# One token tile of an output projection computed by column halves, its second-norm row finished after the expert threshold search, and the route stage ordered by hand

## The chip, the cores and the metric

The kernel runs on one core of one Trainium2 chip. The metric is the device time of one execution in microseconds (us), lower is better. A core has five engines with a queue of instructions each: TensorE (PE in the profile; its weight loads are PEld), VectorE (DVE), ScalarE (ACT), GpSimd (POOL) and SyncE (SP, which here only issues DMAs). Each works through its own queue in order; semaphores tie the queues together.

## The reference, cut to what matters

One layer over 2048 tokens of width 1024, in fp32: a modulated RMS norm, a combined input projection, a convolution half and a neighbourhood-attention half, the output projection with a gated residual, a second modulated RMS norm, and sixteen expert-choice SwiGLU experts of which each takes the 256 tokens with the highest affinity.

```
x = x + g1 * (concatenate([y_conv, y_attn], -1) @ w_out)
h2 = modulate(rms_norm(x, norm_ffn_g), sh2, sc2)           # h * (1 + scale) + shift
aff = softmax(h2 @ w_router)                               # 2048 x 16
wts, tok = top_k(swapaxes(aff, 1, 2), 256)                 # per expert
xs = h2[tok]
y = (silu(xs @ w_gate) * (xs @ w_up)) @ w_down * wts
x = x + g2 * zeros.at[tok].add(y);  out = rms_norm(x, norm_final_g)
```

## The kernel before, in words

`run` calls the stages in turn: `in_proj` (norm, input projection, convolution), `attention`, `route_consts`, `out_proj`, `route`, `moe`. Each matrix product is made of fp32 values split into a high part (a cast, on ACT) and a low part (a subtraction, on DVE or POOL), so that three matmuls stand for one.

**out_proj** goes over 16 token tiles of 128 tokens. `tile_mm(t)` loads the tile of x, runs 48 matmuls of 512 columns into a PSUM tile `po` of two banks (8 slices k, for each of two column halves: high by high, high by low, low by high), multiplies by the gate `rb[:, 0]`, adds x and stores the row tile to `acc`. `norm2(t)` squares with a row sum on ACT (into the tile `h2`) and makes the reciprocal root on POOL (`rstd`, six small instructions). `tail(t)` transposes the tile (eight transposes on TensorE), splits it into `h2h` and `h2l`, and after every second tile runs 16 gate matmuls of 256 columns and makes logits `lg`. `store_h2(t)` scales, adds the shift (`rb[:, 1]`) and stores the row tile to `h2d` in DRAM, from which the experts gather. `soft` makes the softmax of a stretch of slots of `lg`: seven pairs of tiles in the last loop step, the eighth at the end.

**route** transposes the affinities into `pa`, takes a copy `af` and a bf16 copy `afh`, and finds each expert's threshold in 30 steps of a bit search (the loop in L1093 to L1103: a compare with count on DVE, a matmul, three small DVE instructions). Then two masks, a running count `cum`, two transposes into `pt`, and the copy into `slot`.

**moe** goes over 16 experts in 24 chunks of weights each. `prep(e)` makes one-hot tiles from `slot` (16 compares), sums token numbers with them on TensorE, writes `idx`, and has POOL gather rows of `h2d` into `xr` by indirect DMA. `load(i)` brings one megabyte of weights into `raw` (three buffers) from SP and splits it into `whi` and `wlo`; for the first three loads the subtraction is POOL's. `gather` transposes `xr` into the experts' input. The stage begins with `load(0)`, `load(1)`, `load(2)`, `prep(0)` and the four parts of `gather(0)`.

**What sets the order.** The framework's scheduler orders each engine's queue. It plays the program through with its own costs: an engine that is free takes, among the instructions that are ready, the one that stands first in the program; a DMA keeps its issuing engine occupied for the transfer. Inside `tc.manual_schedule(engines=...)` the named engines take that stretch's instructions in program order. That holds for all of `attention`, for ACT, DVE and TensorE (`MAIN`) in `in_proj`, and for POOL (`ENG`) in moe until the fourth chunk. Tiles come from pools that are opened and closed like a stack: `rp` (the route pool, open from before attention to the end), p3a and p3 (attention), p4 (out_proj), p5 (route), p6 (moe, opened when p5 is closed). An instruction waits for the last user of the memory that its tile takes over.

Of the kernel before, what the change touches and what calls it, by code (L numbers as in the profile page):

```python
# [123 lines left out]
class Net:  # L124
# [727 lines left out]
    def out_proj(self):  # L852
        nc, tc, A, S = self.nc, self.tc, self.A, self.S
        with ExitStack() as es:
# [75 lines left out]
            def tile_mm(t):  # L930
# [4 lines left out]
                order = [4, 5, 6, 7, 0, 1, 2, 3]  # L935
                for ki, k in enumerate(order):
                    wh, wl = wo[k]
                    for n in range(2):
                        c = slice(n * 512, (n + 1) * 512)
                        nc.tensor.matmul(po[:, n], hi[:, k], wh[:, c], start=(ki == 0), stop=False)  # L940
                        nc.tensor.matmul(po[:, n], hi[:, k], wl[:, c], start=False, stop=False)
                    for n in range(2):
                        c = slice(n * 512, (n + 1) * 512)
                        nc.tensor.matmul(po[:, n], lo[:, k], wh[:, c], start=False, stop=(ki == KT - 1))
# [3 lines left out]
                sm = [SM[0][:, i, t % 2:t % 2 + 1] for i in range(3)]  # L948
# [4 lines left out]
                XT[t] = (xt, h2, sm, SM[0])  # L953
# [15 lines left out]
            def tail(t):  # L969
                xt, _, _, sm = XT[t]  # L970
                if t % 2 == 0:
                    R[0] = pool.tile([P, KT, W2], F32R, name="h2h", bufs=1)
                    R[1] = pool.tile([P, KT, W2], F32R, name="h2l", bufs=1)
                hh, hl = R[0], R[1]
                q = slice((t % 2) * P, (t % 2 + 1) * P)
                for a in range(2):
                    tp = ps.tile([P, 4, P], F32, name="tp4", bufs=2)
                    for k in range(4):
                        nc.tensor.transpose(tp[:, k, :], xt[:, (4 * a + k) * P:(4 * a + k + 1) * P], self.ident)
                    nc.scalar.copy(hh[:, 4 * a:4 * a + 4, q], tp)  # L980
                    nc.vector.tensor_sub(hl[:, 4 * a:4 * a + 4, q], tp, hh[:, 4 * a:4 * a + 4, q].bitcast(F32))
                if t % 2:
                    pr = ps.tile([2 * E, W2], F32, name="pr")
                    for k in range(KT):
                        nc.tensor.matmul(pr, wrs[:, k], hh[:, k], start=(k == 0), stop=False)
                        nc.tensor.matmul(pr, wrs[:, k], hl[:, k], start=False, stop=(k == KT - 1))
                    lt = pool.tile([2 * E, W2], F32, name="lt", bufs=1)
                    nc.scalar.copy(lt, pr)
                    tl = ps.tile([P, 2, 2, E], F32, name="tl", tag="tl")
                    for i in range(2):  # L990
                        nc.tensor.transpose(tl[:, i].rearrange("p a e -> p (a e)"), lt[:, i * P:(i + 1) * P],
                                            self.ident[:2 * E, :2 * E])
                    lg = self.lg[:, :, t // 2, :]
                    nc.scalar.copy(lg, tl[:, :, 0, :])
                    nc.vector.tensor_add(lg, lg, tl[:, :, 1, :])
                    nc.vector.tensor_mul(lg, lg, sm[:, 1, :, None].to_broadcast([P, 2, E]))
                    nc.vector.tensor_add(lg, lg, lsh[:, None, :].to_broadcast([P, 2, E]))
# [4 lines left out]
            for t in range(NT):  # L1002
                if t % 2 == 0 and t + 2 < NT:
                    ln_a(t // 2 + 1)
                tile_mm(t)
                if t % 2 == 1 and t + 1 < NT:
                    ln_b(t // 2 + 1)
                if t + 1 < NT:
                    ysplit(t + 1)
                if t < NT - 1:  # L1010
                    norm2(t)
                if t:
                    tail(t - 1)
                    store_h2(t - 1)
                if t == NT - 1:
                    self.soft(0, NT // 2 - 1)
            norm2(NT - 1)
            tail(NT - 1)
            self.soft(NT // 2 - 1, NT // 2)
            store_h2(NT - 1)  # L1020

    def route_pool(self, es):
# [5 lines left out]
        self.iob = p.tile([P, CAP], BF16, name="iob")  # L1028

# [44 lines left out]
    def route(self):  # L1074
        nc, tc, A, S = self.nc, self.tc, self.A, self.S
        with ExitStack() as es:
            pool = es.enter_context(tc.tile_pool(name="p5", bufs=1, reuse_waits="tile"))
# [45 lines left out]
            nc.vector.tensor_copy(self.slot.rearrange("p c e -> p (c e)"), pt.rearrange("p b t -> p (b t)"))  # L1123
# [261 lines left out]
```

## Time and profile before

| what | us |
|---|---|
| median of 3 runs | 3349.62 (3347.95 to 3350.89) |
| the profiled execution, whole | 3349.36 |
| its span, first to last instruction | 3347.6 |
| TensorE busy in the span | 3244.6 (97%) |
| DVE busy | 2339.9 (70%) |
| ACT busy | 1659.5 (50%) |
| POOL busy | 414.1 (12%) |

Times in the profile count from the start of the span. In the timeline each row has start, length, engine, source line, operation, output and inputs, and in square brackets how long the engine had been idle and what ended the wait; rows of the same kind that follow each other on an engine are merged (x3). The mean granted clock of TensorE over the span was 0.984 of full speed.

### The profile page before, as it was taken

How to read it: one execution, taken by the hardware profiler on the slowest of the kernel's cores; microseconds unless marked ns; L12 is line 12 of the kernel's file. 1: busy time of each engine (PE TensorE's matmuls, PEld its weight loads, DVE VectorE, ACT ScalarE, POOL GpSimd, SP SyncE). 2: the span in 40 equal slices, each digit the busy share in tenths (PEclk: the TensorE clock that was granted, in tenths of full speed). 3: DMA queues.
4: the chain of work that ended last, by engine and by line, in shares of the span. 5: the costliest groups of instructions: out<-in, count | busy, mean ns of one | idle time of the engine just before them, and what ended most of it. 6: DMA issues, size and time to landing. Idle time of an engine off the chain costs nothing. (4 is left out here: it accounts for less than half of the span.)

```text
span 3347.6 us, 47930 instructions
## 1 busy us (share of the span) xinstructions
PE 3244.6 (97%) x18394; PEld 2751.2 (82%) x18394; DVE 2339.9 (70%) x3637; ACT 1659.5 (50%) x2784; POOL 414.1 (12%) x739
## 2 busy tenths in 40 slices
PE   7999998999999699999999999999999999999998
PEld 4788887999777588888888888888888888888786
DVE  6798987998666776566665766756666566575666
ACT  7211124889433355454554555545545455454554
POOL 3100002444211200000000000000000000001221
PEclk9999998999999699999999999999999999999999
DMA  6243329996433466555565555665556556556765
GB/s 233 76 135 130 112 96 241 258 239 158 147 131 109 168 218 210 193 202 198 200 210 197 198 200 196 208 201 198 196 199 211 196 196 213 187 205 226 265 246 193
DMA packets 159585, 635.61 MB, mean 190 GB/s; under 512 B 47926, under 2 KB 62678, under 8 KB 106108
## 3 DMA queue, kind: packets, MB, share of 16 engines
q1 hardware_dynamic: 138172, 542.68, 46.1%
q0 software_dynamic: 21184, 89.86, 11.1%
q8 instruction: 145, 2.38, 0.3%
q14 instruction: 84, 0.69, 0.1%
HBM read 560.38 MB, written 72.10 MB: 189 GB/s over the span
## 5 line engine op out<-in xcount | busy, mean ns | idle before, releaser
L1227 PE MATMUL pgu<-xt,whi 128*128 128x512 f32 x4096 | 1446.1, 398 | 0.5 <-DVE xt L1197 0.5
L208 DVE TENSOR_TENSOR wlo<-raw,whi 128x1024 fp32r<-128x1024 f32 x762 | 918.9, 1220 | 648.6 <-ACT whi L207 647.2
L1228 PE MATMUL pgu<-xt,wlo 128*128 128x256 f32 x4096 | 1150.3, 281 | 1.4 <-DVE wlo L208 1.4
L207 ACT CAST whi<-raw 128x1024 fp32r<-128x1024 f32 x768 | 793.0, 1050 | 564.2 <-PE py L1263 278.4
L1227 PEld LDWEIGHTS pgu<-xt,whi 128*128 128x128 f32 x4096 | 769.8, 188 | 187.9 <-DVE xt L1197 0.9
L1228 PEld LDWEIGHTS pgu<-xt,wlo 128*128 128x128 f32 x4096 | 774.5, 189 | 2.9 <-DVE wlo L208 2.3
L1259 PE MATMUL py<-whi,hh 128*128 128x512 f32 x1024 | 405.9, 396 | 0.0
L1260 PE MATMUL py<-wlo,hh 128*128 128x512 f32 x1024 | 400.3, 391 | 0.0
L1263 PE MATMUL py<-whi,hl 128*128 128x512 f32 x1024 | 315.9, 390 | 0.0
L528 DVE SCALAR_TENSOR_TENSOR cacc<-v,k,cacc 128x2048 f32<-128x2048 f32 x120 | 281.5, 2346 | 1.6
L1232 ACT COPY gt<-pgu 128x256 f32<-128x256 f32 x512 | 188.9, 369 | 177.6 <-PE pgu L1228 177.6
L465 PE MATMUL mm<-hhi,whi 128*128 128x512 f32 x576 | 227.6, 395 | 0.0
L1263 PEld LDWEIGHTS py<-whi,hl 128*128 128x128 f32 x1024 | 192.4, 188 | 41.6
L467 PE MATMUL mm<-hhi,wlo 128*128 128x512 f32 x576 | 224.8, 390 | 0.0
L1259 PEld LDWEIGHTS py<-whi,hh 128*128 128x128 f32 x1024 | 192.7, 188 | 39.0 <-issue 0.2
L466 PE MATMUL mm<-hlo,whi 128*128 128x512 f32 x576 | 224.7, 390 | 0.0
L1260 PEld LDWEIGHTS py<-wlo,hh 128*128 128x128 f32 x1024 | 192.8, 188 | 38.2 <-issue 0.2
L1233 DVE TENSOR_TENSOR gt<-pgu,gt 128x256 f32<-128x256 f32 x512 | 213.5, 417 | 7.0 <-ACT gt L1232 6.9
L207 ACT CAST hh<-sl 128x256 fp32r<-128x256 f32 x256 | 104.1, 407 | 224.2 <-DVE sl L1236 223.8
L1315 POOL DMA_INDIRECT acc<-y,idx x28 | 51.9, 1854 | 1261.9 <-DVE y L1313 1184.9
L728 DVE CUSTOM_DVE_ANT_0 pt<-sp,bi 128x640 f32<-128x640 f32 (+1 forms) x128 | 113.5, 887 | 29.4 <-PE sp L721 27.8
L208 DVE TENSOR_TENSOR hl<-sl,hh 128x256 fp32r<-128x256 f32 x256 | 108.8, 425 | 34.1 <-ACT hh L207 7.1
(307 smaller groups left out, 4121.8 us busy)
## 6 DMA issues: line engine op xcount, KB each, us to landing
raw<-w_gu SPq DMA_DIRECT2D x256, 1024.0 KB, 4.8
raw<-w_dn SPq DMA_DIRECT2D x128, 1024.0 KB, 4.8
bi<-bias SPq DMA_DIRECT2D x14, 960.0 KB, 4.9
wm<-wm POOLq DMA_DIRECT2D x24, 512.0 KB, 4.2
vb<-vd SPq DMA_DIRECT2D x119, 96.0 KB, 9.5
wraw<-w_in SPq DMA_DIRECT2D x20, 512.0 KB, 4.5
kh<-kh POOLq DMA_DIRECT2D x16, 576.0 KB, 9.4
kl<-kl POOLq DMA_DIRECT2D x16, 576.0 KB, 10.6
```

The source lines that it names most:

```text
L207: nc.scalar.copy(hi, full)
L208: (eng or nc.vector).tensor_sub(lo, full, hi.bitcast(F32))
L465: nc.tensor.matmul(ps, w[0][:, k, :], h[0][:, k, :], start=(k == 0), stop=False)
L466: nc.tensor.matmul(ps, w[0][:, k, :], h[1][:, k, :], start=False, stop=False)
L467: nc.tensor.matmul(ps, w[1][:, k, :], h[0][:, k, :], start=False, stop=(k == KT - 1))
L528: nc.vector.scalar_tensor_tensor(acc, v[:, w:w + T], cwt[:, j, w:w + 1], acc, op0=OP.mult, op1=OP.add)
L1227: nc.tensor.matmul(p_, hi[:, a, k], xt[:, k, :], start=(k == 0), stop=False)
L1228: nc.tensor.matmul(p_[:, :CAP], lo[:, a, k], xt[:, k, :CAP], start=False, stop=(k == KT - 1))
L1233: nc.vector.tensor_add(t[:, a], pg[a][:, :CAP], t[:, a])
L1259: nc.tensor.matmul(py[e][a][b], hh[:, sa], hi[:, ff, sb], start=(f == 0), stop=False)
L1260: nc.tensor.matmul(py[e][a][b], hh[:, sa], lo[:, ff, sb], start=False, stop=False)
L1263: nc.tensor.matmul(py[e][a][b], hl[:, sa], hi[:, ff, sb], start=False, stop=(f == 15))
```

## The change

The last token tile's projection is computed by column halves: all of k for the first 512 columns into one PSUM tile, then the eight transposes of the tile before it, then all of k for the other 512 into a second PSUM tile. The functions are cut up for that (`proj`, `tile_in`, `flip`, `gates`, `logits`), and a new `last_pair` writes out the order of the last two tiles for TensorE, DVE and ACT. The square of the last tile is taken by halves. Its second-norm row is scaled into a tile `h3` while the last softmax runs; the shift is added and the row stored to `h2d` in `route`, after the search, and the tile `shift` moves with `h3` into the route pool (8 KB of a partition). `route` is ordered by hand too: `afh` is copied ahead of `af`, and the copy into `slot` goes to ACT. `soft` takes each step for both halves of the batch. The DMA descriptor scratch is set to 4096 bytes.

```diff
-            rb = pool.tile([P, 3, D], F32, name="rb")
-            for i in range(3):
-                nc.sync.dma_start(rb[:, i], S["rows"][i:i + 1, :].to_broadcast([P, D]))
+            rb = pool.tile([P, 2, D], F32, name="rb")
+            for i, r in enumerate((rb[:, 0], self.shift, rb[:, 1])):
+                nc.sync.dma_start(r, S["rows"][i:i + 1, :].to_broadcast([P, D]))
...
+            def proj(po, hi, lo, n):
+                order = [4, 5, 6, 7, 0, 1, 2, 3]
+                for ki, k in enumerate(order):
+                    wh, wl = wo[k]
+                    for m in n:
+                        c = slice(m * 512, (m + 1) * 512)
+                        nc.tensor.matmul(po[:, m], hi[:, k], wh[:, c], start=(ki == 0), stop=False)
+                        nc.tensor.matmul(po[:, m], hi[:, k], wl[:, c], start=False, stop=False)
+                    for m in n:
+                        c = slice(m * 512, (m + 1) * 512)
+                        nc.tensor.matmul(po[:, m], lo[:, k], wh[:, c], start=False, stop=(ki == KT - 1))
...
-                for c in ((slice(0, 512), slice(512, D)) if t == NT - 1 else (slice(0, D),)):
-                    nc.vector.tensor_mul(h2[:, c], po.rearrange("p a b -> p (a b)")[:, c], rb[:, 0, c])
-                    nc.vector.tensor_add(xt[:, c], xt[:, c], h2[:, c])
+            def tile_mm(t):
+                xt, hi, lo, po, h2 = tile_in(t)
+                proj(po, hi, lo, (0, 1))
+                nc.vector.tensor_mul(h2, po.rearrange("p a b -> p (a b)"), rb[:, 0])
+                nc.vector.tensor_add(xt, xt, h2)
...
-                nc.vector.scalar_tensor_tensor(h2, xt, sm[1], rb[:, 2], op0=OP.mult, op1=OP.mult)
-                nc.vector.tensor_add(h2, h2, rb[:, 1])
+                nc.vector.scalar_tensor_tensor(h2, xt, sm[1], rb[:, 1], op0=OP.mult, op1=OP.mult)
+                nc.vector.tensor_add(h2, h2, self.shift)
...
+            def flip(t, a):
...
+                return lambda: nc.vector.tensor_sub(hl[:, 4 * a:4 * a + 4, q], tp, hh[:, 4 * a:4 * a + 4, q].bitcast(F32))
+
+            def gates(pr, ks, kinds=(0, 1)):
+                for k in ks:
+                    for z in kinds:
+                        nc.tensor.matmul(pr, wrs[:, k], R[z][:, k], start=(k == 0 and z == 0),
+                                         stop=(k == KT - 1 and z == 1))
...
+            def last_pair():
+                t = NT - 1
+                xt, hi, lo, po, h2 = tile_in(t)
+                sm = XT[t][2]
+                sq = pool.tile([P, 2], F32, name="sq")
+                c = [slice(0, 512), slice(512, D)]
+
+                def square(q):
+                    nc.scalar.activation(h2[:, c[q]], xt[:, c[q]], AF.Square, accum_out=sq[:, q:q + 1])
+
+                def half(po, q):
+                    nc.vector.tensor_mul(h2[:, c[q]], po[:, q], rb[:, 0, c[q]])
+                    nc.vector.tensor_add(xt[:, c[q]], xt[:, c[q]], h2[:, c[q]])
+
+                proj(po, hi, lo, (0,))
+                for a in range(2):
+                    flip(t - 1, a)()
+                half(po, 0)
+                square(0)
+                po1 = ps.tile([P, 2, 512], F32, name="po", bufs=2)
+                proj(po1, hi, lo, (1,))
+                store_h2(t - 1)
+                self.soft(0, NT // 2 - 1)
+                low0 = flip(t, 0)
+                half(po1, 1)
+                nc.sync.dma_start(S["acc"][t * P:(t + 1) * P], xt)
+                square(1)
+                low0()
+                pr = ps.tile([2 * E, W2], F32, name="pr")
+                low1 = flip(t, 1)
+                gates(pr, range(KT // 2))
+                nc.vector.tensor_add(sm[0], sq[:, 0:1], sq[:, 1:2])
+                nc.vector.tensor_scalar(sm[0], sm[0], 1.0 / D, EPS, op0=OP.mult, op1=OP.add)
+                self.rstd(*sm)
+                low1()
+                gates(pr, range(KT // 2, KT), (0,))
+                gates(pr, range(KT // 2, KT), (1,))
+                logits(t, pr)
+
+                def scaled(q):
+                    nc.vector.scalar_tensor_tensor(self.h3[:, q], xt[:, q], sm[1], rb[:, 1, q], op0=OP.mult, op1=OP.mult)
+
+                self.soft(NT // 2 - 1, NT // 2, (lambda: scaled(c[0]), lambda: scaled(c[1])))
...
-            for t in range(NT):
+            for t in range(NT - 1):
...
-                if t < NT - 1:
-                    norm2(t)
+                norm2(t)
-                if t == NT - 1:
-                    self.soft(0, NT // 2 - 1)
-            norm2(NT - 1)
-            tail(NT - 1)
-            self.soft(NT // 2 - 1, NT // 2)
-            store_h2(NT - 1)
+            with tc.manual_schedule(engines=MAIN):
+                last_pair()
...
+        self.shift = p.tile([P, D], F32, name="shift")
+        self.h3 = p.tile([P, D], F32, name="h3")
...
-    def soft(self, s0, s1):
+    def soft(self, s0, s1, fill=()):
         nc = self.nc
+        lg = [self.lg[:, b, s0:s1] for b in range(2)]
+        mx = [self.mx[:, b, s0:s1] for b in range(2)]
+        bc = [m[:, :, None].to_broadcast([P, s1 - s0, E]) for m in mx]
         for b in range(2):
-            lg, mx = self.lg[:, b, s0:s1], self.mx[:, b, s0:s1]
-            bc = mx[:, :, None].to_broadcast([P, s1 - s0, E])
-            nc.vector.tensor_reduce(mx, lg, axis=AX.X, op=OP.max)
-            nc.vector.tensor_sub(lg, lg, bc)
-            nc.scalar.activation(lg, lg, AF.Exp)
-            nc.vector.tensor_reduce(mx, lg, axis=AX.X, op=OP.add)
-            nc.vector.reciprocal(mx, mx)
-            nc.vector.tensor_mul(lg, lg, bc)
+            nc.vector.tensor_reduce(mx[b], lg[b], axis=AX.X, op=OP.max)
+        for b in range(2):
+            nc.vector.tensor_sub(lg[b], lg[b], bc[b])
+            nc.scalar.activation(lg[b], lg[b], AF.Exp)
+        for f in fill[:1]:
+            f()
+        for b in range(2):
+            nc.vector.tensor_reduce(mx[b], lg[b], axis=AX.X, op=OP.add)
+        for b in range(2):
+            nc.vector.reciprocal(mx[b], mx[b])
+        for b in range(2):
+            nc.vector.tensor_mul(lg[b], lg[b], bc[b])
+        for f in fill[1:]:
+            f()
 
     def route(self):
         nc, tc, A, S = self.nc, self.tc, self.A, self.S
         with ExitStack() as es:
+            es.enter_context(tc.manual_schedule(engines=MAIN))
...
+            afh = pool.tile([P, 2 * P], BF16, name="afh")
+            nc.vector.tensor_copy(afh, pf.bitcast(BF16)[:, 1::2])
             af = pool.tile([P, 2 * P], F32, name="af")
             nc.scalar.copy(af, pf)
-            afh = pool.tile([P, 2 * P], BF16, name="afh")
-            nc.vector.tensor_copy(afh, pf.bitcast(BF16)[:, 1::2])
...
             for b in range(2):
                 nc.tensor.transpose(pt[:, b], cum[:, 0, b * P:(b + 1) * P], self.ident)
-            nc.vector.tensor_copy(self.slot.rearrange("p c e -> p (c e)"), pt.rearrange("p b t -> p (b t)"))
+            nc.vector.tensor_add(self.h3, self.h3, self.shift)
+            nc.sync.dma_start(S["h2d"][T - P:], self.h3)
+            nc.scalar.copy(self.slot.rearrange("p c e -> p (c e)"), pt.rearrange("p b t -> p (b t)"))
...
-    nc = bacc.Bacc("TRN2", target_bir_lowering=False, num_devices=1, dynamic_dma_scratch_size=8192)
+    nc = bacc.Bacc("TRN2", target_bir_lowering=False, num_devices=1, dynamic_dma_scratch_size=4096)
```

## Rows read from the trace of the kernel before

**Rows 1.** Windows (length, engines' busy us, clock, DMA share, GB/s), the experts.

```profile
1150.00:3340.00 2190.00, 2176.77 (x11908) 1859.28 (x11906) 1423.99 (x2229) 1161.48 (x1881) 154.76 (x200) 1.00 0.60 207
```

**Rows 2.** Timeline (start, length in us), search's end to first expert matmul.

```profile
1123.32 0.42 DVE L1119 TENSOR_TENSOR cum<-cum 128x256 f32<-128x256 f32 x1
...
1124.51 0.33 SPq L1143 DMA_DIRECT2D g<-bm  x1
...
1124.52 0.42 DVE L1123 COPY slot<-pt 128x256 f32<-128x256 f32 x1 [0.78 <-PE pt L1122]
...
1129.19 0.15 DVE L1174 SCALAR_TENSOR_TENSOR idx<-ax 128x2 int32<-128x2 f32 x1
...
1130.19 1.12 POOL L1182 DMA_INDIRECT xr<-h2d,idx  x1 [24.84 <-issue]
...
1139.55 0.79 PE L1227 MATMUL pgu<-xt,whi 128*128 128x512 f32 x1 [0.55 <-DVE xt L1197]
```

**Rows 3.** Timeline: last `h2` store, first weight loads, casts, subtractions.

```profile
1083.83 0.32 SPq L965 DMA_DIRECT2D h2d<-h  x1
1084.24 1.70 SPq L1210 DMA_DIRECT2D raw<-w_gu  x3
...
1090.38 1.99 ACT L207 CAST whi<-raw 128x1024 fp32r<-128x1024 f32 x2 [2.46 <-DMA raw<-w_gu]
...
1091.50 13.85 POOL L208 TENSOR_TENSOR wlo<-raw,whi 128x1024 fp32r<-128x1024 f32 x6 [0.96 <-ACT whi L207]
...
1092.88 1.99 ACT L207 CAST whi<-raw 128x1024 fp32r<-128x1024 f32 x2 [0.51 <-DMA raw<-w_gu]
```

**Rows 4.** Timeline of DVE, last token tile to the search's first step.

```profile
1069.70 0.45 DVE L1067 TENSOR_REDUCE mx<-lg 128x7 f32<-128x112 f32 x2
...
1071.30 0.45 DVE L1072 TENSOR_TENSOR lg<-lg,mx 128x112 f32<-128x112 f32 x2
...
1074.93 1.29 DVE L950 TENSOR_TENSOR h<-po,rb 128x512 f32<-128x512 f32 x2 [3.17 <-PE po L944]
...
1080.79 1.28 DVE L963 SCALAR_TENSOR_TENSOR h<-xt,sm,rb 128x1024 f32<-128x1024 f32 x1 [0.56 <-POOL sm L199]
...
1084.79 0.19 DVE L995 TENSOR_TENSOR lg<-lg,tl 128x32 f32<-128x32 f32 x1 [0.98 <-ACT lg L994]
...
1088.41 0.48 DVE L1096 TENSOR_SCALAR_CACHE_REDUCE junk<-afh,cand 128x256 bf16<-128x256 bf16 x1
```

**Rows 5.** Groups of instructions by form, POOL (busy us, mean ns of one).

```profile
L208 POOL TENSOR_TENSOR wml<-wm,wmh 128x1024 fp32r<-128x1024 f32 x3 | 8.0, 2672 | 10.4 <-ACT wmh L207 7.3 <-PE pm L392 3.2
```

**Rows 6.** Timeline of TensorE, end of the projection to the last gate matmul.

```profile
1068.67 0.63 PE L944 MATMUL po<-wo,ylo 128*128 128x512 f32 x2
...
1074.26 0.63 PE L944 MATMUL po<-wo,ylo 128*128 128x512 f32 x2
...
1074.73 1.04 PE L979 MATMUL tp<-ident,xt 128*128 128x128 f32 x8
...
1078.07 1.72 PE L979 MATMUL tp<-ident,xt 128*128 128x128 f32 x8 [2.31 <-DVE h2l L981]
...
1083.44 0.28 PE L986 MATMUL pr<-h2l,wrs 128*32 128x256 f32 x1
```

**Rows 7.** Timeline of POOL, ACT and DVE, from in_proj into attention.

```profile
506.88 0.53 POOL L700 DMA_DIRECT2D kh<-kh  x1 [129.34 <-PE mm L467]
...
512.79 0.51 POOL L700 DMA_DIRECT2D kl<-kl  x1 [5.38 <-PE tp L505]
...
534.62 0.59 ACT L508 CAST v<-tp 128x512 bf16<-128x512 f32 x1 [9.81 <-DMA vd<-v]
...
556.94 0.06 DVE L1035 MEMSET slot<- 128x1 bf16 x1
```

**Rows 8.** DMA queues, 524 to 530 us (packets, MB, share of 16 engines).

```profile
q0 software_dynamic: 179, 1.20, 85.4%
q1 hardware_dynamic: 179, 0.14, 21.8%
```

More of the change, by code (lines that the diff above doesn't have):

```diff
@@ L934, in tile_mm @@
                 po = ps.tile([P, 2, 512], F32, name="po", bufs=2)
[L935 to L944, printed above, removed]
                 h2 = pool.tile([P, D], F32, name="h2", tag="h2", bufs=2)
@@ L947, in tile_mm @@
                     SM[0] = pool.tile([P, 3, 2], F32, name="sm4", bufs=2)
-                sm = [SM[0][:, i, t % 2:t % 2 + 1] for i in range(3)]
-                for c in ((slice(0, 512), slice(512, D)) if t == NT - 1 else (slice(0, D),)):
-                    nc.vector.tensor_mul(h2[:, c], po.rearrange("p a b -> p (a b)")[:, c], rb[:, 0, c])
-                    nc.vector.tensor_add(xt[:, c], xt[:, c], h2[:, c])
+                XT[t] = (xt, h2, [SM[0][:, i, t % 2:t % 2 + 1] for i in range(3)], SM[0])
+                return xt, hi, lo, po, h2
+            def tile_mm(t):
[3 more added lines that the diff above has]
+                nc.vector.tensor_add(xt, xt, h2)
                 nc.sync.dma_start(S["acc"][t * P:(t + 1) * P], xt)
-                XT[t] = (xt, h2, sm, SM[0])
             def norm2(t):
@@ L962, in store_h2 @@
                 xt, h2, sm, _ = XT.pop(t)
-                nc.vector.scalar_tensor_tensor(h2, xt, sm[1], rb[:, 2], op0=OP.mult, op1=OP.mult)
-                nc.vector.tensor_add(h2, h2, rb[:, 1])
+                nc.vector.scalar_tensor_tensor(h2, xt, sm[1], rb[:, 1], op0=OP.mult, op1=OP.mult)
+                nc.vector.tensor_add(h2, h2, self.shift)
                 nc.sync.dma_start(S["h2d"][t * P:(t + 1) * P], h2)
             R, SM, XT = {}, {}, {}
-            def tail(t):
-                xt, _, _, sm = XT[t]
-                if t % 2 == 0:
+            def flip(t, a):
+                xt = XT[t][0]
+                if t % 2 == 0 and a == 0:
                     R[0] = pool.tile([P, KT, W2], F32R, name="h2h", bufs=1)
@@ L975, in tail @@
                 q = slice((t % 2) * P, (t % 2 + 1) * P)
-                for a in range(2):
[L977 to L981, printed above, removed]
+                tp = ps.tile([P, 4, P], F32, name="tp4", bufs=2)
@@ new lines, in flip @@
+                for k in range(4):
+                    nc.tensor.transpose(tp[:, k, :], xt[:, (4 * a + k) * P:(4 * a + k + 1) * P], self.ident)
+                nc.scalar.copy(hh[:, 4 * a:4 * a + 4, q], tp)
+                return lambda: nc.vector.tensor_sub(hl[:, 4 * a:4 * a + 4, q], tp, hh[:, 4 * a:4 * a + 4, q].bitcast(F32))
[4 more added lines that the diff above has]
+                                         stop=(k == KT - 1 and z == 1))
@@ new lines, in logits @@
+            def logits(t, pr):
+                sm = XT[t][3]
+                lt = pool.tile([2 * E, W2], F32, name="lt", bufs=1)
+                nc.scalar.copy(lt, pr)
+                tl = ps.tile([P, 2, 2, E], F32, name="tl", tag="tl")
+                for i in range(2):
+                    nc.tensor.transpose(tl[:, i].rearrange("p a e -> p (a e)"), lt[:, i * P:(i + 1) * P],
+                                        self.ident[:2 * E, :2 * E])
+                lg = self.lg[:, :, t // 2, :]
+                nc.scalar.copy(lg, tl[:, :, 0, :])
+                nc.vector.tensor_add(lg, lg, tl[:, :, 1, :])
+                nc.vector.tensor_mul(lg, lg, sm[:, 1, :, None].to_broadcast([P, 2, E]))
+                nc.vector.tensor_add(lg, lg, lsh[:, None, :].to_broadcast([P, 2, E]))
@@ L982, in tail @@
+            def tail(t):
+                for a in range(2):
+                    flip(t, a)()
                 if t % 2:
                     pr = ps.tile([2 * E, W2], F32, name="pr")
[L984 to L996, printed above, removed]
@@ L997, in tail @@
-                    nc.vector.tensor_add(lg, lg, lsh[:, None, :].to_broadcast([P, 2, E]))
+                    gates(pr, range(KT))
+                    logits(t, pr)
[33 more added lines that the diff above has]
+                gates(pr, range(KT // 2, KT), (1,))
+                logits(t, pr)
+                def scaled(q):
+                    nc.vector.scalar_tensor_tensor(self.h3[:, q], xt[:, q], sm[1], rb[:, 1, q], op0=OP.mult, op1=OP.mult)
+                self.soft(NT // 2 - 1, NT // 2, (lambda: scaled(c[0]), lambda: scaled(c[1])))
```

2 lines of the change are left out of this document (1 added, 1 removed).

## The prediction

> **What bounds the kernel now.** I read the windows first. From 1150 us on, TensorE is busy for 2176.8 of 2190 us: sixteen experts at the higher clock level, 137 us each, and nothing of the change lies there [rows 1]. So the change counts by one thing alone: when the first expert's first matmul starts.
>
> The timeline from the end of the threshold search to that matmul shows its chain [rows 2]. DVE ends the addition of `cum` at 1123.74 (1123.32 + 0.42; I call this point E). TensorE transposes `cum`, DVE copies it to `slot` at 1124.52, one-hot compares and matmuls follow, `idx` is written at 1129.19, POOL issues the first gather at 1130.19 (E + 6.45), and 9.36 us later the matmul starts (1139.55). SP's row at 1124.51 shows how its queue behaves: the load of `g` lies over `cum` and left only when the transposes had read it.
>
> Then I asked what had to be done by 1130. POOL's program order inside moe is: subtract `wlo` for loads 0, 1 and 2 (six instructions), then the gather. [Rows 3] show how that is hidden today: SP stores the last `h2` row at 1083.83 and issues the three weight loads right behind it, ACT casts from 1090.38, POOL subtracts from 1091.50 for 13.85 us without a gap. All of it runs under the search and is over 25 us before it is needed. This cover is what the change touches.
>
> **The change part by part.**
>
> *Behind the search (the term that decides).* Two engines get an instruction of route that today is not in their queues.
>
> First, ACT: `slot` is now copied by ACT, after the transposes. Pool p6 of moe opens after p5 of route is closed, and the scheduler deals p6's tiles out only after p5's last reader, which is TensorE's transpose of `cum` (in the compiled program of before the first weight load is listed right behind the `slot` copy). So the casts into `whi` come behind the `slot` copy in ACT's queue. Today ACT has nothing there that waits for the search, so the casts run at 1090.38. Afterwards none can start before the copy is done: E + 0.78 (1124.52 less E) + 0.42 = E + 1.2. POOL's first subtraction starts 1.12 us after the first cast does [rows 3], so at E + 2.3; six of them end at E + 16.2, and only then comes the gather. That alone is 9.7 us late.
>
> Second, SP: the store of `h3` waits for an addition of 128x1024 on DVE that follows `cum` (1.28 us at most, by the pass of that size at L963 [rows 4]), so it issues at E + 1.3. Its place in SP's queue is by program order among what is ready whenever the scheduler's SP is free. The scheduler has load 0 ready when the transposes end (0.7 us after E by [rows 2]) and the store at 1.28, so load 0 goes first; while it is occupied with that megabyte the store becomes ready and goes before loads 1 and 2. On the chip load 0 then issues early as now, and loads 1 and 2 stand behind a store that waits for the end of the search. [Rows 3] price what follows, for it is the same sequence: from the store (1083.83) to the cast of the load next behind it (1090.38) are 6.55 us. So: store E + 1.3, cast of load 1 at E + 7.85, POOL on it at E + 8.97 (load 0's two subtractions are done by then), four subtractions of 2.31 us end at E + 18.2, gather at E + 18.25 against E + 6.45. **+11.8 us.** Bounds: 9.7, if loads 1 and 2 stand ahead of the store; 16.4, if load 0 stands behind it too (E + 8.97 + 13.85 = E + 22.8).
>
> The addition of the shift itself costs nothing on DVE: it lies under the transposes and the `slot` copy, which today end at 1124.94, E + 1.2, and it ends at E + 1.28. The store's landing costs nothing either while the gather is this late; without the delay it would land 2.5 us (the step from 1090.38 to 1092.88, one load) before E + 7.85, in time for E + 6.45.
>
> A POOL subtraction of the same size took 2.67 us elsewhere [rows 5]; four at that price add 1.4 us, my upper bound. The Trainium skill ("SBUF — State Buffer", Who interferes with whom) says that POOL shares a port pair with DVE and blocks fully while DVE runs an instruction with two SBUF inputs or in a two-port mode. The subtractions now run beside one-hot compares, so by it the sum would be some 1.4 us longer; the six under the search ran beside a DVE that was as busy, at 2.31.
>
> *Ahead of the search.* TensorE does the same 48 matmuls, with the eight transposes of tile 14 (1.04 us) moved between the halves. That lets DVE begin early: four steps of k, 24 matmuls, take 5.6 us (1068.67 to 1074.26 [rows 6]), so the first half closes at about 1069.3. But on DVE the hand order puts behind it what today fills idle time: two subtractions, multiply and add of half 0, `store_h2(14)` (1.28 + 1.2) and soft of the first seven slots (2.05, from 1069.70 to 1071.75) [rows 4]. From 1070.6 (transposes and cast first) that makes 1.3 + 1.2 + 2.4 + 2.05 = 1077.55, then half 1 in 1.25: tile 15 is complete at 1078.8, against 1077.4 today (from 1074.93, two passes of 1.29 with little overlap). From there today's chain takes 7.4 us to the logits (1084.79), with `store_h2(15)`'s 1.28 in front of the last subtraction. Without it, and with the first half's part done: four transposes at the rate of today's later ones (0.86, eight in 1.72, where the earlier eight took 1.04), the sixteen gate matmuls (an estimate of 3.2, between the later transposes' 0.215 each, 3.4, and the earlier ones' 0.13, 2.1), and 1.07 to the logits (from 1083.72): 5.3 with the steps between, so logits at 1084.1, 0.7 early. Then `scaled` of half 0 puts 0.4 into soft, and `afh` no longer waits for ACT's copy of `af` (0.45 back). **-0.8 us.** Bounds: -2.2, with TensorE at the rate of the earlier transposes throughout; +3, if the hand-ordered stretch made the first half wait for tile 13's gate matmuls, between which it is threaded today. I exclude most of that: instructions outside such a stretch slip between its own (DVE's L1035 ran inside the hand-ordered attention [rows 7]). The search itself, the order in its loop and the 30 steps, stays as it is.
>
> *Memory.* `shift` and `h3` add 8 KB to the route pool, which opens before attention, so all of attention's tiles lie 8 KB further up over in_proj's. Today the first load of `kh` needs other tiles released than the load of `kl`, which waits until 512.79 for `hhi0` [rows 7]; 8 KB higher `kh` lies over `hhi0` as well, so its 0.59 MB leave at 512.79, into a stretch where DMA is full and where ACT waited 9.81 us, and DVE with it, for a store of `vd` (cast at 534.62). [Rows 8] show why that store is slow: 179 packets of POOL's queue against 179 of SP's. With some 80 more packets of POOL's ahead, at 30 a microsecond, the store lands 2.7 us later, less 0.9 when the small packets come: **+1.7 us.** The Trainium skill ("DMA: Bandwidth & Descriptors", Queues, rings and completion order) says that each DMA engine goes round the queues packet by packet; the equal counts agree. A single queue in order would make it the whole 0.59 MB, 2.7. Bounds 0 and 2.7.
>
> *The rest.* Loading `shift` instead of a third of `rb` is the same transfer. The descriptor scratch is halved; no row shows a wait for it, and POOL's gathers run an expert (137 us) ahead, which would hide one. 0 us.
>
> **Sum.** Against the profiled 3349.36 (span 3347.6 and 1.8 around it; the median 3349.62 is 0.3 above): 1.7 - 0.8 + 11.8 = 12.7, so 3362.0 us.
>
> **The rivals.**
> - *ACT only*: loads 1 and 2 stand ahead of the store. For it: a scheduler that gives all three loads out at once. Against: it spaces them (in the compiled program of before fifteen one-hot compares are listed between loads 0 and 1). 1.7 - 0.8 + 9.7: 3360.0 us.
> - *All three loads behind the store*: if the scheduler has the addition done before p5 is free. 1.7 - 0.8 + 16.4: 3366.7 us.
> - *Not slower*: the weight chain stays under the search. It needs the casts ahead of the `slot` copy in ACT's queue and the loads ahead of the store; it decides once POOL's six subtractions end before E + 6.45, that is, begin before E - 7.4. For it: [rows 3] show 25 us of slack, so even a partial escape would do. Against: nothing of p6 can be dealt out before p5 is read to its end. 1.7 - 0.8: 3350.3 us.
> - *The region as a barrier*, +3 on top of the forecast: 3365 us.
>
> **How the numbers follow.** The forecast 0.55, ACT only 0.16, all three behind 0.13, barrier 0.04, not slower 0.12. The forecast's own range, from the bounds, is 3359.0 (0 - 2.2 + 11.8) to 3368. With ACT only at its lower bounds and all three behind, 8 in 10 lie within 3356 to 3368. A change of 0.2% (6.7 us, about what a measurement of this kernel can tell from none) sets the line at 3356.3: every delayed case is above it, so slower 0.87; the not-slower case splits into same 0.11 and faster 0.02, which would need the early gains at their bound and no cost in attention.
>
> **What would show it.** Right: ACT's first cast into `whi` just behind its copy of `slot`, POOL's subtractions after the search and not under it, SP's second weight load behind the store of `h3`, the first gather 13 us after `idx` (11 with ACT only), the search starting within 1 us of today's place, ACT's wait for `vd` near 11.5. Wrong: casts at 1090 as now, or a first gather within 1 us of `idx`. The forecast fails most easily in the queue orders, which no row shows, and there first in SP's.

## The result, and the profile after

The changed kernel took 3370.94 us (median of 6 runs, 3368.94 to 3379.46) against 3350.26 for the kernel before on the same chip: a ratio of 1.0059, 95% interval 1.0048 to 1.0070. It is slower, as forecast, but by 20.7 us and not by 12.7: 3 us above the range of the forecast, which ended at 3368.

The profiled execution is the longest of the six (span 3377.7). Of its excess 6.6 us are there already at POOL's first bias load, in the input projection, where executions of the same code differ: that load starts at 525.1 in it and at 518.5 to 522.0 in the profiled executions of the other kernels (e1 apart, where it comes late for another reason, told below). So the stages are compared from landmark to landmark, not by the clock on the left.

**Behind the search.** The timeline of the changed kernel from the end of the search (E = 1135.74 + 0.42) to the first expert matmul; it answers to [rows 2, 3].

```profile
1135.74 0.42 DVE L1186 TENSOR_TENSOR cum<-cum 128x256 f32<-128x256 f32 x1
1136.94 0.37 ACT L1192 COPY slot<-pt 128x256 f32<-128x256 f32 x1 [36.21 <-PE pt L1189]
1137.21 1.99 ACT L207 CAST whi<-raw 128x1024 fp32r<-128x1024 f32 x2
1137.32 0.32 SPq L1191 DMA_DIRECT2D h2d<-h  x1
1137.69 17.18 SPq L1279 DMA_DIRECT2D raw<-w_gu  x5
1138.34 4.77 POOL L208 TENSOR_TENSOR wlo<-raw,whi 128x1024 fp32r<-128x1024 f32 x2 [34.99 <-ACT whi L207]
1144.16 1.99 ACT L207 CAST whi<-raw 128x1024 fp32r<-128x1024 f32 x2 [4.96 <-DMA raw<-w_gu]
1145.28 9.23 POOL L208 TENSOR_TENSOR wlo<-raw,whi 128x1024 fp32r<-128x1024 f32 x4 [2.18 <-DMA raw<-w_gu]
1147.63 2.31 DVE L1243 SCALAR_TENSOR_TENSOR idx<-ax 128x2 int32<-128x2 f32 x1
1154.69 1.12 POOL L1251 DMA_INDIRECT xr<-h2d,idx  x1 [0.18 <-issue]
1164.22 3.67 PE L1263 MATMUL tp<-ident,xr 128*128 128x128 f32 x16 [6.25 <-DMA xr<-h2d,idx]
1168.44 0.79 PE L1296 MATMUL pgu<-xt,whi 128*128 128x512 f32 x1 [0.55 <-DVE xt L1266]
```

The queues stand as forecast. ACT sat 36 us in front of the `slot` copy and casts right behind it; SP's five loads follow the store. POOL's last four subtractions end at E + 18.35 and the gather leaves at E + 18.53 (forecast 18.25, before 6.45). What was not forecast is the gap after it: TensorE has the gathered rows 9.5 us after the gather, where it was 4.56, and the matmul follows the gather by 13.75, not 9.36. The row of the kernel before, which [rows 2] leave out (gather at 1130.19):

```profile
1134.75 1.97 PE L1194 MATMUL tp<-ident,xr 128*128 128x128 f32 x8 [1.65 <-DMA xr<-h2d,idx]
```

**Attention's start.** POOL's loads (`kh` and `kl` are the high and low part of a head's keys, `bi` its bias tiles) and ACT's waits (`vd` holds the values in DRAM), first the changed kernel, then the kernel before; [rows 7] hold before's first `kh` load and its one wait for `vd`.

```profile
519.39 0.54 POOL L700 DMA_DIRECT2D kh<-kh  x1 [135.27 <-PE tp L505]
525.09 0.57 POOL L666 DMA_DIRECT2D bi<-bias  x1 [2.54 <-PE mm L467]
542.45 0.58 ACT L508 CAST v<-tp 128x512 bf16<-128x512 f32 x1 [11.04 <-DMA vd<-v]
547.42 1.11 POOL L666 DMA_DIRECT2D bi<-bias  x2
548.52 0.54 POOL L700 DMA_DIRECT2D kh<-kh  x1
563.93 0.58 ACT L508 CAST v<-tp 128x512 bf16<-128x512 f32 x1 [7.72 <-DMA vd<-v]
569.01 1.28 ACT L736 ACT_TABLE_LOAD   x1
586.52 0.45 SPq L867 DMA_DIRECT2D shift<-rows  x1
```

```profile
518.49 0.57 POOL L666 DMA_DIRECT2D bi<-bias  x1 [3.13 <-PE mm L467]
539.52 0.57 POOL L666 DMA_DIRECT2D bi<-bias  x1
555.59 0.55 POOL L666 DMA_DIRECT2D bi<-bias  x1 [15.49 <-DVE v L515]
556.12 0.54 POOL L700 DMA_DIRECT2D kh<-kh  x1
556.28 1.28 ACT L736 ACT_TABLE_LOAD   x1
```

The first wait for `vd` is 11.04 us, near the 11.5 forecast. But there is a second, of 7.72. Before, the third bias load waited 15.49 us for a tile of `in_proj`; 8 KB higher it waits for nothing, leaves with the second, and the second `kh` load behind it. Together, as I read the order of the rows, they stand in the way of a store of `vd`; the runs with 8 and with 2.5 KB below test that, though not which of the two loads does it. From the first bias load to the table load (the start of the softmaxes) it is 43.92 us, before 37.79. The last row above shows one more: `shift`, no longer a tile of out_proj, is loaded early in attention (before at 843.79, with the rest of `rb`).

**The last tile.** DVE and TensorE of the changed kernel from tile 14's product to the search; it answers to [rows 4, 6].

```profile
1074.48 1.22 DVE L956 TENSOR_TENSOR h<-po,rb 128x1024 f32<-128x1024 f32 x1 [3.56 <-PE po L940]
1092.12 0.69 DVE L1027 TENSOR_TENSOR xt<-xt,h 128x512 f32<-128x512 f32 x1
1093.54 0.28 PE L990 MATMUL pr<-h2l,wrs 128*32 128x256 f32 x1
1096.70 0.19 DVE L1003 TENSOR_TENSOR lg<-lg,tl 128x32 f32<-128x32 f32 x1 [1.78 <-ACT lg L1002]
1100.39 0.48 DVE L1163 TENSOR_SCALAR_CACHE_REDUCE junk<-afh,cand 128x256 bf16<-128x256 bf16 x1
```

From tile 14's product to E it is 61.7 us (1136.16 less 1074.48), before 63.3 (1123.74 less 1060.42). Tile 15 is complete 18.3 us after that product, and 18.4 was forecast (1078.8 less 1060.42).

### The profile page after: what moved, and what is told of

It is laid out like the page before. It is cut to its first block, busy times and chain, and to the rows that moved or that the text cites. A ratio compares the mean times of both kernels' runs of the same rounds, so it can differ in the third digit from the quotient of the medians.

```text
span 3377.7 us, 47934 instructions
## 1 busy us (share of the span) xinstructions
PE 3244.7 (96%) x18394; PEld 2750.3 (81%) x18394; DVE 2354.3 (70%) x3638; ACT 1659.3 (49%) x2787; POOL 412.9 (12%) x739
```

## The experiments

Each kernel was timed against the kernel before in five rounds on one chip, but not all on the same: the kernel before took 3350.26 us beside the changed kernel, 3349.88 beside e1 to e4, 3350.21 beside e5 to e8, 3350.47 beside e9 to e11 and 3352.04 beside e12. So kernels of different groups are compared by their ratios. From the first expert matmul to the end of the span, work that none of these edits is about, the fourteen profiled executions took 2203.3 to 2209.3 us; terms of 1 or 2 us are therefore read from the stages and not from the medians. The table gives, for one profiled execution of each (e1 stands under *Memory*), the stages by the starts of their rows: *attention* from POOL's first bias load to ACT's table load; *heads* from there to the cast of `iti`; *tile* from tile 14's product to E; *gather* after E; *rows* from the gather to TensorE's first transpose of them; *matmul* after E.

| kernel | median us | ratio (95%) | attention | heads | tile | gather | rows | matmul |
|---|---|---|---|---|---|---|---|---|
| before | 3350.26 | 1 | 37.8 | 286.7 | 63.3 | 6.45 | 4.6 | 15.8 |
| changed | 3370.94 | 1.0059 (1.0048 to 1.0070) | 43.9 | 287.9 | 61.7 | 18.5 | 9.5 | 32.3 |
| e2 scratch | 3348.93 | 0.9997 (0.9988 to 1.0006) | 37.2 | 286.5 | 63.8 | 6.45 | 4.4 | 15.8 |
| e3 slot on DVE | 3369.86 | 1.0061 (1.0047 to 1.0075) | 41.6 | 286.7 | 62.7 | 18.6 | 9.0 | 31.8 |
| e4 store late | 3371.47 | 1.0062 (1.0049 to 1.0075) | 40.9 | 288.0 | 63.6 | 19.0 | 6.5 | 29.7 |
| e5 both | 3360.32 | 1.0029 (1.0020 to 1.0038) | 42.0 | 288.4 | 62.8 | 7.5 | 9.2 | 21.6 |
| e6 hold | 3364.88 | 1.0041 (1.0028 to 1.0054) | 40.7 | 287.0 | 62.9 | 18.5 | 4.4 | 28.1 |
| e7 early | 3348.14 | 0.9996 (0.9988 to 1.0005) | 37.1 | 286.5 | 62.3 | 6.5 | 4.5 | 15.9 |
| e8 8 KB | 3353.08 | 1.0012 (1.0001 to 1.0022) | 40.3 | 286.3 | 64.1 | 6.5 | 4.6 | 15.7 |
| e9 2.5 KB | 3351.22 | 0.9997 (0.9987 to 1.0007) | 39.1 | 286.4 | 63.3 | 6.5 | 4.4 | 15.6 |
| e10 both, six | 3357.73 | 1.0018 (1.0009 to 1.0027) | 41.1 | 288.2 | 62.8 | 7.5 | 4.5 | 16.7 |
| e11 early, ACT | 3361.50 | 1.0037 (1.0023 to 1.0051) | 37.0 | 287.1 | 62.5 | 19.0 | 6.5 | 29.8 |
| e12 shift held | 3352.86 | 0.9999 (0.9990 to 1.0008) | 44.7 | 286.5 | 61.3 | 7.5 | 4.4 | 16.6 |

**Which queue holds the chain (e3, e4, e11).** e3 is the changed kernel with

```diff
-            nc.scalar.copy(self.slot..., pt...)
+            nc.vector.tensor_copy(self.slot..., pt...)
```

> The changed kernel with the copy to slot back on DVE (after the shift of h3), so that ACT's casts have nothing in front that waits for the search. Theory, as in the prediction: SP's store of h3, ahead of weight loads 1 and 2, holds the chain alone; casts of load 0 move under the search, POOL's subtractions of load 0 too, the four of loads 1 and 2 still end 18 us after E and the first gather leaves at E + 18.3; time as the changed kernel within 1 us (3370). Rival (ACT's queue is what costs): gather at E + 7 to 9, some 9 us or more faster than the changed kernel (3361 or less).

e4 is the changed kernel with the store moved from `route` into `moe`:

```diff
             load(2)
+            nc.sync.dma_start(S["h2d"][T - P:], self.h3)
             prep(0)
```

> The changed kernel with the store of h3 issued behind weight load 2 in SP's queue; slot stays on ACT. Theory, the prediction's bound with ACT only: loads 1 and 2 land under the search, all casts come behind the slot copy, POOL's six subtractions run without a gap from E + 2.3 and the gather leaves at E + 16.2, 2.1 us sooner; 3368.8 within 1 us. Rival (SP's queue is what costs): gather within 1 us of E + 6.5, time 12 us or more below the changed kernel (3359 or less).

Both rivals fall: neither entry alone is "the" cause, each is enough. With `slot` on DVE two of the six subtractions went under the search and the gather still left at E + 18.55 (E = 1129.35), because the store holds loads 1 and 2. POOL of e3:

```profile
1096.39 4.64 POOL L208 TENSOR_TENSOR wlo<-raw,whi 128x1024 fp32r<-128x1024 f32 x2
1138.48 9.25 POOL L208 TENSOR_TENSOR wlo<-raw,whi 128x1024 fp32r<-128x1024 f32 x4 [37.45 <-DMA raw<-w_gu]
```

With the store out of the way it left at E + 19.02, later and not 2.1 us sooner as expected. Its timeline (DVE and POOL after E = 1130.60) says why; the last row is the compares of the kernel before:

```profile
1131.79 15.84 DVE L1230 TENSOR_SCALAR oh<-iob,slot 128x256 bf16<-128x256 bf16 x16
1132.78 13.99 POOL L208 TENSOR_TENSOR wlo<-raw,whi 128x1024 fp32r<-128x1024 f32 x6 [34.97 <-ACT whi L207]
1148.63 0.15 DVE L1242 SCALAR_TENSOR_TENSOR idx<-ax 128x2 int32<-128x2 f32 x1
1149.62 1.12 POOL L1250 DMA_INDIRECT xr<-h2d,idx  x1 [2.86 <-issue]
```

```profile
1124.98 3.22 DVE L1162 TENSOR_SCALAR oh<-iob,slot 128x256 bf16<-128x256 bf16 x16
```

The sixteen one-hot compares, 3.22 us before, take 15.84 beside the subtractions, so `idx` comes only after them and POOL waits 2.86 us more. e11 repeats it on e7 (below), with `slot` back on ACT as the one difference:

> The run with the last h2 row finished ahead of the search, with one change: slot copied by ACT. So of the changed kernel's two queue entries only ACT's is left, with the store, the memory and SP's order undisturbed. Theory (either entry alone holds the chain, and the rest is not additive): casts from E + 1.1, POOL's six subtractions till E + 16.2, DVE's idx held beside them till E + 17 or later, gather at E + 18 to 19, and loads 3 to 5 (whose buffers come free only then) beside it, first matmul at E + 28 to 30; 12 to 14 us above that run, 3360 to 3362. Rival (my bound with ACT only, no contention): gather at E + 16.2, matmul at E + 25.5, 3357.8. Rival (ACT's entry alone is harmless): 3348.

It came out as expected: gather at E + 19.0, matmul at E + 29.8, and 13.4 us above e7.

**Both undone (e5), and the loads beside the gather (e6, e10).** e5 is e4 with `slot` copied by DVE, ahead of the shift.

> The changed kernel with both undone: slot copied by DVE ahead of the shift of h3, and the store of h3 behind weight load 2 in SP's queue. Theory (the queues' order is the cause, the shift itself is nearly free): casts and POOL's six subtractions under the search, idx at E + 6.7 (one pass of 1.22 us later than in the kernel before, since the shift now stands in front of the one-hots), gather at E + 7.7, first expert matmul at E + 17 instead of E + 32; 15 us below the changed kernel, about 3355.5, with the 5 to 7 us at attention's start left. Rival (the gather waits for the landing of the late store, or the shift costs more than it hides): gather at E + 10 or later, 3358 or more.

The gather left at E + 7.47 as expected, but the rows were late again, and the time was 5 us above the expectation. SP, POOL and TensorE of e5, E = 1132.99:

```profile
1135.36 0.33 SPq L1394 DMA_DIRECT2D h2d<-h  x1
1135.80 1.64 SPq L1278 DMA_DIRECT2D raw<-w_gu  x3
1140.46 1.12 POOL L1250 DMA_INDIRECT xr<-h2d,idx  x1 [26.61 <-DVE oh L1230]
1149.63 1.97 PE L1262 MATMUL tp<-ident,xr 128*128 128x128 f32 x8 [6.27 <-DMA xr<-h2d,idx]
```

I had cleared the store's way for loads 0 to 2 and left 3 to 5 behind it. They left 4.7 us ahead of the gather. e6 takes the changed kernel and holds the transfers beside its gather:

```diff
+                if i == 5:
+                    nc.scalar.copy(raw[:, 0, :1], XR[0][1][:, :1])
                 nc.sync.dma_start(raw, src)
...
+                    nc.scalar.copy(g2[:, :1], XR[0][1][:, :1])
                     nc.sync.dma_start(g2, A["bm2"][3:4, :].to_broadcast([P, D]))
...
+                            nc.scalar.copy(gf[:, :1], XR[0][1][:, :1])
                             nc.sync.dma_start(gf, A["ngf"].to_broadcast([P, D]))
```

> The changed kernel with weight load 5 and the loads of g and gf made to wait till the second gather has landed (ACT writes one column of their tiles from the gathered rows first); queue orders as in the changed kernel. Theory (these 2 MB on the same DMA engines slow the gather): gather leaves at E + 18.5 as now, TensorE's first transpose of its rows 4.6 us later (as before the change) and not 9.5; first matmul at E + 27.4 against E + 32.3, 5 us below the changed kernel, 3366. Rival (the transposes wait for something else, such as the one-hots on DVE): E + 32, no difference (3370.5).

e10 is e5 with the loads 3 to 5 issued, by a function `fetch`, in front of the store:

```diff
             load(2)
+            for i in (3, 4, 5):
+                RAW[i] = fetch(i)
             nc.sync.dma_start(S["h2d"][T - P:], self.h3)
```

> As the run with both undone, but with weight loads 3, 4 and 5 also ahead of the store of h3 in SP's queue (their buffers come free under the search). Theory (in that run these 3 MB, held back by the store, ran beside the gather and cost its rows 4.6 us): gather at E + 7.5 as there, first transpose of its rows 4.6 to 6 us later and not 9.2, first matmul at E + 17 to 18.4 instead of E + 21.6; 3.2 to 4.6 us below that run, 3356 to 3357. Rival (the landing of the store itself, or the one-hots, set the gather's rows): no difference, 3360.

In e6 the rows came 4.4 us after the gather, and the median is 6.1 us below the changed kernel's; in e10 they came after 4.5, and the median is 2.6 below e5's. The intervals of each pair of ratios overlap, so it is the rows that decide here and not the medians. The windows from the gather to the rows (changed kernel, then e6; the last two columns are DMA share and GB/s):

```profile
1154.70:1164.20 9.50, 2.87 (x30) 1.85 (x30) 5.92 (x33) 0.00 (x0) 2.17 (x2) 0.50 0.86 319
```

```profile
1147.50:1152.00 4.50, 2.96 (x31) 1.95 (x32) 3.79 (x23) 0.00 (x0) 2.19 (x2) 0.50 0.53 137
```

So the loads that come late delay the gather a second time, as traffic. The Trainium skill ("DMA: Bandwidth & Descriptors", Queues, rings and completion order) lets a DMA engine go round its queues packet by packet; that the rows took 9.5 us beside SP's loads and 4.4 without them agrees, though no row shows the order of the packets.

**Memory (e1, e2, e8, e9).** e1 is the kernel before with

```diff
+        self.pad = p.tile([P, 2 * D], F32, name="pad")
+        self.nc.gpsimd.memset(self.pad[:, :8], 0.0)
```

in `route_pool`; e2 is the kernel before with scratch 4096.

> The kernel before, with 8 KB of padding (one tile that is not used) at the end of the route pool, so that attention's tiles lie as in the changed kernel; nothing else differs. Theory, from the two traces: 3356.3 to 3357.6 us (6 to 7.3 above the kernel before), and in the trace the first kh load waits till in_proj's last hhi0 use, the third bias load and the second kh load of POOL leave some 8 us earlier against in_proj's end than before, and ACT waits a second time for a store of vd, about 7 us. Rival 1, my forecast: 1.7 above the kernel before, one wait for vd of 11.5 us. Rival 2: the whole early delay belongs to the one execution that was profiled: no difference (3350).

> The kernel before with the descriptor scratch halved to 4096, nothing else. Theory: no difference, 3350 within 1.5 us, since all addresses move by the same 4 KB and POOL's transfers wait for the eighth before them as they did. Rival: POOL's queue finds less room for descriptors at the start of attention and the early delay (up to 6 us, 3356) comes from there.

e2 made no difference. e1 was a badly made probe: 3376.65 us, ratio 1.0078 (1.0065 to 1.0091), more than the whole change. One row shows it: its memset had to wait for `in_proj` to free the memory, and all of attention's loads stood behind it in POOL's queue.

```profile
543.56 0.10 POOL L1030 MEMSET pad<- 128x8 f32 x1 [164.41 <-PE mm L466]
```

e8 writes the padding by DVE at the end of `route_consts`, after attention; e9 is e8 with 640 columns (2.5 KB).

> The kernel before with 8 KB of padding in the route pool, as before, but the padding is written only after attention (by DVE), so that nothing of it stands in POOL's queue ahead of attention's loads. Theory: 5 to 7 us above the kernel before, 3355 to 3357, with kh behind hhi0's last use, the third bias load and the second kh load 8 us earlier than before, and a second wait of ACT for a store of vd of some 7 us. Rival 1 (my forecast): 1.7 us above, 3351.5, one wait. Rival 2: no difference (3350).

> The kernel before with 2.5 KB of padding in the route pool instead of 8 (written after attention, as there): kh then lies over hhi0 and waits for it, but the third bias tile still lies over the tile that held its load back before. Theory (the forecast's 1.7 was the kh load alone, the rest of what 8 KB cost comes from the third bias load and the second kh load leaving early): the third bias load again behind DVE's last v, from POOL's first bias load to ACT's table load 37.5 to 39 us (37.2 to 37.8 at the old place, 40.3 with 8 KB), 3350.5 to 3352. Rival (the late kh is what costs): as with 8 KB, 40 us or more, 3353 or more.

POOL and ACT of e8, then of e9:

```profile
542.60 1.11 POOL L666 DMA_DIRECT2D bi<-bias  x2
554.67 0.58 ACT L508 CAST v<-tp 128x512 bf16<-128x512 f32 x1 [3.29 <-DMA vd<-v]
559.75 1.28 ACT L736 ACT_TABLE_LOAD   x1
```

```profile
541.75 0.57 POOL L666 DMA_DIRECT2D bi<-bias  x1
557.62 0.55 POOL L666 DMA_DIRECT2D bi<-bias  x1 [15.30 <-DVE v L515]
558.32 1.28 ACT L736 ACT_TABLE_LOAD   x1
```

With 8 KB the third bias load goes with the second and ACT waits a second time (3.29 us); with 2.5 KB it waits as before, and no second wait follows. By time e8 is 2.9 us above the kernel before, less than the 5 to 7 expected, and its interval (0.3 to 7.4) does not tell that from the 1.7 of the forecast; the second wait in the trace does. By the trace the stage takes 40.3 to 44.7 in the eight executions with the 8 KB shift (mean 41.9), 39.1 with 2.5 KB (39 was the upper end expected) and 37.0 to 37.8 in four without (mean 37.3). So 8 KB cost 4.6 on the mean (3.0 in e8, the one kernel in which they are the only difference), and the late `kh` alone, in one execution, 1.8.

**The early load of shift (e12).** e10 with one instruction at the end of `route_consts`:

```diff
+        nc.vector.tensor_copy(self.shift[:, :8], self.iob[:, :8])
```

> The run with both undone and six loads ahead of the store, with the load of shift made to wait till attention is over (DVE writes its first columns from iob first), so that it leaves where the load of rb left before the change. Theory (in the changed kernel the load of shift, whose tile is no longer one of out_proj's, leaves 8 to 20 us into attention and costs there, since SP issues it between the loads of the second pair of heads): from ACT's table load to the cast of iti 286.3 to 287.1 us, as in all kernels with rb whole (286.3 to 287.1 in six of them), against 288.2 in the run that this one differs from by this alone, 1 to 1.9 us below that run, 3356. Rival (the 1 to 2 us between kernels here are only scatter, or come from the 8 KB): 287.9 or more, no difference (3357.7).

The load moved to 853.63, and *heads* fell to 286.5 as expected. Of the six executions with the early load four lose 1.2 to 1.8 us against the kernel before, all between 29 and 44 us after the table load, where the second head begins, and two lose nothing or 0.3; the seven others scatter from 286.3 to 287.1. The mean is 1.15 us. In three of the four (e4, e5, e10) TensorE waits there 1.30 to 1.70 us for a load of the second head, `qs`, which POOL issued 5.4 to 5.8 us after SP issued that of `shift`; the changed kernel has no such row and loses its 1.2 in smaller waits. SP and TensorE of e10, then SP of e12:

```profile
576.68 0.45 SPq L867 DMA_DIRECT2D shift<-rows  x1
598.28 0.41 PE L719 MATMUL sp<-kh,qs 128*128 128x384 f32 x1 [1.30 <-DMA qs<-ql]
```

```profile
853.63 0.33 SPq L867 DMA_DIRECT2D shift<-rows  x1
```

Against the kernel before, the ratio went from 1.0018 to 0.9999, which is more than this stage explains. By the terms summed up below e12 should even be 4.1 us above the kernel before (4.6 for the memory, -1.3 for the tile, 0.8 to the matmul), and its interval is 3.4 below to 2.7 above. There the terms don't close. In its profiled execution the stretch behind the first expert matmul took 2203.3 us, against 2206.3 in e10 and 2208.1 in the kernel before; why stays open.

**The last tile with nothing else (e7).** The changed kernel without `shift` and `h3` in the route pool, `slot` on DVE, scratch 8192, and the row finished before the search:

```diff
+                def shifted(q):
+                    nc.vector.tensor_add(h2[:, q], h2[:, q], rb[:, 2, q])
+
+                scaled(c[0])
+                scaled(c[1])
                 logits(t, pr)
-                self.soft(NT // 2 - 1, NT // 2, (lambda: scaled(c[0]), lambda: scaled(c[1])))
+                self.soft(NT // 2 - 1, NT // 2, (lambda: shifted(c[0]), lambda: shifted(c[1])))
+                nc.sync.dma_start(S["h2d"][T - P:], h2)
```

> The column halves and the hand order of the changed kernel, but the last h2 row is finished ahead of the search: its two scalings in DVE's wait for the last logits, its two shifts in the gaps of the softmax, its store ahead of weight load 0; shift and h3 out of the route pool (memory as in the kernel before), slot copied by DVE, scratch 8192. Theory: attention's start as before (0), search start 0.3 to 2.2 us sooner after tile 14's product than the 28.0 of the kernel before, gather at E + 6.45: 3348 to 3349.6, just below the kernel before. Rival (the 8 KB are not what costs at attention's start, or the halves cost by themselves): 3352 or more.

3348.14 us, 2 below the kernel before, not to be told from it (0.9996, 0.9988 to 1.0005). It has the lowest median of all kernels here: the row's work fits into DVE's gaps ahead of the search, so there is nothing to move behind it.

## Why the prediction was wrong in size and right in kind

**Step by step.** *Queue orders*: right, +12.1 measured where +11.8 was forecast, by the steps named (cast of load 1 at E + 8.0, forecast 7.85), and e3 shows that SP's store alone gives the same gather time. *From gather to matmul*: this step failed. I read 9.36 us from [rows 2] and kept it as a constant. I priced loads 0 to 2 and never asked about loads 3 to 5, which before had left under the search (SP issued all six from 1084.24 to 1105.70): with three buffers in `raw` they must follow the delayed ones, and so come beside the gather. It became 13.75 (+4.4), and e6 and e10 give it back. *Memory*: the mechanism was half seen, and the step is mis-sized. I followed the first load that would come later (`kh`), and not those that would come earlier; the term measured 4.6, forecast 1.7 with an upper bound of 2.7. *"Loading `shift` ... is the same transfer ... 0 us"*: failed. The bytes are the same, the time at which they leave is not (+1.15). *Ahead of the search*: right, -1.3 on the mean (62.5 in seven executions of the new order with `shift` behind the search, 63.8 in five of the old, e1's 64.5 among them), forecast -0.8, the 61.3 to 63.6 of single ones within the bounds. No barrier was seen: tile 15 came where forecast.

The sum, 12.1 + 4.4 + 4.6 + 1.15 - 1.3 = 20.95, meets the 20.7 measured. Most of the miss, 8 us, is the traffic (4.4) and the memory (2.9). That it meets so closely is in part luck: the terms come from single executions or from means that scatter by 1 to 4 us, and for e12 the same terms miss by 4.

**The signs named.** ACT's casts, POOL's subtractions, SP's second load and ACT's first wait were as named. Not as named: `idx` to gather 7.1 us, not 13, since `idx` was held up too; and the search started 12.0 us later on the clock, 6.6 of it from the input projection.

**The rivals.** *ACT only*, priced at 9.7, could not have come out so: e11 has that case alone and costs 13.4, with `idx` late by the port and the rows late by traffic. *All three loads behind the store* fell: ACT cast load 0 right behind its copy of `slot`, without a wait for the load, and POOL began on it at E + 2.2, so load 0 had gone ahead of the store. *Not slower* and *barrier* fell.

## What to carry to other kernels

When a chain of loads is pushed behind a wait, price the delay twice: once for the queue, and once for what the late transfers now run beside. When tiles move in memory, list which loads come free earlier as well as which come later: an early transfer in a full stretch can cost as much as a late one. A small piece of work is worth moving only after one has looked for gaps where it stands; here DVE had them.

## What the runs showed of the hardware

POOL's subtractions stopped DVE, not the other way about. In the changed kernel `idx`, 0.15 us before, took 2.31, the length of one subtraction, and six of e4's compares reached TensorE 2.30 us apart, the subtractions' pace. The subtractions themselves took 2.31 us each there (9.23 for four) as they had before (13.85 for six). The Trainium skill ("SBUF — State Buffer", Who interferes with whom) says that whoever issues first has the shared port pair for its whole instruction and the other blocks; this agrees, and the forecast, which took only the half of the rule in which DVE is first, had put the cost on POOL alone. The search's own compares, which write an accumulator and which that section exempts, did not suffer: from its first compare to E it took 35.3 us before, with 13.85 us of subtractions beside it, and 35.8 after, without them.

TensorE's clock went with the size of the gain on the last tile. In the windows of the last gate matmuls (changed kernel, then e4; the clock stands ahead of the DMA share) the same code was granted 1.00 and 0.50, that is 2.4 and 1.2 GHz, after the same pause of 2.70 us (the first row of each pair shows it). From tile 14's product to the logits it took 22.2 us in the changed kernel (1096.70 less 1074.48) and 24.2 in e4 (1091.17 less 1067.00), and *tile* is 63.6 there against 61.7. The other executions of this order fall in line: from tile 14's product to the last gate matmul e12 was granted 1.00 and has 22.2 and 61.3, e3, e5, e6 and e10 were granted 0.92 and have 23.3 to 23.5 and 62.7 to 62.9, and e4 was granted 0.89. Why the clock fell after that pause in some executions and not in others no run shows.

```profile
1092.95 0.63 PE L983 MATMUL tp<-ident,xt 128*128 128x128 f32 x4 [2.70 <-DVE xt L1027]
1093.20:1095.80 2.60, 2.43 (x20) 1.72 (x18) 1.21 (x4) 1.02 (x4) 1.38 (x6) 1.00 0.81 271
```

```profile
1085.50 1.09 PE L983 MATMUL tp<-ident,xt 128*128 128x128 f32 x4 [2.70 <-DVE xt L1027]
1086.10:1090.10 4.00, 3.90 (x19) 2.80 (x17) 1.00 (x3) 0.61 (x3) 1.51 (x6) 0.50 1.00 340
```
